# Sample tokens of a hybrid decoder layer: convolution states moved as whole rows, memory attention with four heads in 32-column strips

## The chip, the cores and the metric

The kernel runs on one core of one Trainium2 chip. The metric is the device time of one execution in microseconds (us). The engines are named as in the profile: PE (TensorE matmul), PEld (TensorE weight load), DVE (VectorE), ACT (ScalarE), POOL (GpSimd, which also issues the gathers of expert rows) and SP (SyncE, which issues all other DMAs, one after another in the order of its program). L12 is line 12 of the kernel before, unless a line of the changed kernel is named.

## The reference

One decoder layer with shared weights for 1024 prompt tokens and 8 sample tokens. The change concerns the sample tokens alone:

```python
def _causal_dwconv(u, buf, w, b):
    full = jnp.concatenate([buf.astype(u.dtype), u], axis=1)
    out = lax.conv_general_dilated(full, w[:, None, :], (1,), 'VALID', ..., feature_group_count=u.shape[-1])
    return out + b, full[:, full.shape[1] - (w.shape[0] - 1):]
...
xbc_c, new_ssd_buf = _causal_dwconv(xbc, ssd_buf, ssd_conv_w, ssd_conv_b)        # 3 old rows, 3072 channels
cv, new_conf_buf = _causal_dwconv(glu, conf_buf, conf_conv_w, conf_conv_b)       # 30 old rows, 1024 channels
sc = jnp.einsum('blhd,bmhd->bhlm', qh, mem_k) * (MEM_HEADDIM ** -0.5)            # 4 heads of 256, 256 memory tokens
pr = jax.nn.softmax(sc, axis=-1)
o = jnp.einsum('bhlm,bmhd->blhd', pr, mem_v)
```

For each sample token both convolutions read a state of old rows and give back the state shifted by one row with the new row at its end. In the memory attention each of the 8 samples has keys and values of its own (4 heads, 256 tokens, 256 features: 1 MB of keys and 1 MB of values per sample).

## The kernel before, in words

The prompt runs in four groups of 128, 128, 384 and 384 tokens (called G0 to G3 here). `main(G)` works on feature-major blocks of 128 features: each product loads a 512 KB block of weights into the pool `wr` (four buffers, `load_raw`, L167) and multiplies it. In G2 and G3 the block is first split on chip into two float32r parts by ACT (`wh`, L175) and DVE (`wl`, L177), so that its buffer is free again after the split; the products with `wso`, `wmo` and `wco` use it raw on PE (L197).

Between the products the program emits, at a fixed pace, rows of the expert layer of earlier groups: POOL gathers a 512 KB set of expert vectors into `uv` (L404), DVE multiplies them (L413, L423). The order of every engine's queue is fixed when the program is built; nothing is reordered at run time.

The sample tokens ride with G1 in the input projection (their columns land in `proj_s`). The rest of their first half, `samples()`, is a generator. Its first step runs behind G1, one step more after each input product of G2, and what is left over is emitted by `drain()` in the first half of G3 (L565). A scheduler then moves what it can forward: the first convolution's steps stand in the queues of G1's memory attention.

- First convolution (L880 to L896): three pieces of 8 channel blocks. Each loads the old rows into `win[..., 0:3]`, POOL writes the new row into `win[..., 3]`, DVE does four taps, and SP stores `win[..., 1:4]`. In `win` a row of a channel and a sample has four floats, in memory three, so that each load and store moves runs of 12 bytes: 128 x 64 of them, 96 KB.
- Second convolution (L943 to L955): eight blocks with 31 taps; `wn` holds 31 floats where memory holds 30, so that runs are 120 bytes, 128 x 8 per transfer.
- Memory attention (`sample_attention`, L970): for each head and sample a 256 KB load into the pool `sb` (four buffers), then two products of an 8-column block with 256 columns (`zq` holds a sample's query in one column and zeros in the others, so that the samples' products add up in one PSUM tile of 8 partitions). Heads go in pairs: scores of 16 loads, softmax over 8 partitions, then the values likewise.

On the chip the first convolution runs from about 691 us, the second from 1578 us, the keys from 1669 us. The values' products, and all but three of their loads, stand in G3 at 2320 to 2356 us.

Of the kernel before, what the change touches and what calls it, by code (L numbers as in the profile page):

```python
# [18 lines left out]
P = 128  # L19
D = 1024  # L20
# [47 lines left out]
def hybrid_layer(ctx: ExitStack, tc, I, O):  # L68
# [145 lines left out]
    def tick(n=1, work=bg):  # L214
        """Emits the next n steps of the work that fills the gaps."""
# [19 lines left out]
    def behind():  # L235
        """The vector engine's instruction LAG before the last that is not one of the experts' rows."""
# [7 lines left out]
    def spread():  # L244
        """Emits the experts' next rows that are due, behind the vector engine's work up to here."""
# [50 lines left out]
    def layer_norm_f(xs, nt):  # L296
        """Centres and scales feature-major blocks in place."""
# [22 lines left out]
    def route(pn, ntb, heads, sv, si, idx, gate, ij=None):  # L320
        """sv, si: for each half [pn, ntb, heads, 16], the best keys; idx, gate [pn, ntb, heads*16]."""
# [21 lines left out]
        # gates  # L343
# [9 lines left out]
        # ranks in both halves from the position: a < 4: a*16 + b; a >= 4: 64 + (a-4)*4 + b  # L353
# [33 lines left out]
    def layer_norm2(r, pn, junk, rows=None):  # L387
        """Token-major [pn, D] in place: the last normalisation."""
# [18 lines left out]
    def peer_experts(pn, ns, x1, idx, gate, acc):  # L407
        """acc [pn, D] = sum over the ns slots of gate * gelu(x1 . u) * v."""
# [33 lines left out]
    def front(g):  # L442
        """Loads a group's tokens, splits them, and works out the step sizes of its state space."""
# [6 lines left out]
        G.nx = nx = nt + NS if g == RIDE else nt    # the sample tokens ride with an early group  # L450
        G.no = nt + NS if G.last else nt            # and, from their mixers on, with the last
# [35 lines left out]
    def out_product(G, src, xs, f, name, add=False):  # L487
        """An output block; the sample columns go to S[name]."""
# [11 lines left out]
    def pack(G, srcs, scale=None, s=None):  # L500
        """The operands of an output product, in the last group with the sample columns s behind them."""
# [12 lines left out]
    def main(G):  # L514
# [24 lines left out]
        # -- state space branch, the convolution branch's blocks between its products  # L539
        ms, squares = None, []  # L540

        def sums(n):
            """The sums over the squares of the first n quarters."""
# [49 lines left out]
        # -- attention to the memory  # L593
# [50 lines left out]
        # -- the convolution branch's rest  # L644
# [8 lines left out]
        # -- output projection and residual  # L653
# [12 lines left out]
    def norm1(G):  # L666
        """The first normalisation."""
# [6 lines left out]
    def keep_tokens(G):  # L674
        """Token-major copies for the experts."""
# [9 lines left out]
    def routing(G):  # L685
        """The tokens' experts and gates, in steps."""
# [37 lines left out]
    def softplus_dt(ps, pn, nt):  # L724
        """dt = softplus(ps + bias), da = -exp(a_log) * dt; [pn, nt, 32]."""
# [10 lines left out]
        dve.scalar_tensor_tensor(w, u, -1.0, e, op0=OP.add, op1=OP.subtract)   # (u-1) - e  # L736
# [119 lines left out]
    def sample_mixers():  # L856
        # step sizes
# [21 lines left out]
        # convolution of x, B, C  # L879
# [3 lines left out]
        for j0 in (0, 8, 16):  # L883
            js = slice(j0, j0 + 8)
            win = sb()[:, :256].rearrange("p (j b t) -> p j b t", j=8, b=8)
            sp.dma_start(win[:, :, :, 0:3], I["sconv"][:, js])
            pool.tensor_copy(win[:, :, :, 3], proj_s[:, 16 + j0:24 + j0])
            for i in range(4):
                w = cw[:, js, i].unsqueeze(2).to_broadcast([P, 8, 8])
                if i == 0:  # L890
                    dve.tensor_tensor(xc[:, js], win[:, :, :, 0], w, op=OP.mult)
                else:
                    dve.tensor_tensor(tmp[:, js], win[:, :, :, i], w, op=OP.mult)
                    dve.tensor_tensor(xc[:, js], xc[:, js], tmp[:, js], op=OP.add)
            sp.dma_start(O["sconv"][:, js], win[:, :, :, 1:4])
            yield  # L896
# [4 lines left out]
        # state update  # L901
# [40 lines left out]
        # convolution branch  # L942
# [3 lines left out]
        cv = proj_s[:, 40:48]  # L946
        for j in range(8):
            wn = sb()[:, :8 * TAPS].rearrange("p (b t) -> p b t", b=8)
            sp.dma_start(wn[:, :, 0:30], I["fconv"][:, j])
            dve.tensor_tensor(wn[:, :, 30], proj_s[:, 40 + j], sg[:, j], op=OP.mult)  # L950
            sp.dma_start(O["fconv"][:, j], wn[:, :, 1:31])
            pr = sb()[:, :8 * TAPS].rearrange("p (b t) -> p b t", b=8)
            dve.tensor_tensor(pr, wn, cw_[:, j].unsqueeze(1).to_broadcast([P, 8, TAPS]), op=OP.mult)
            dve.tensor_reduce(cv[:, j], pr, axis=AX.X, op=OP.add)
            yield  # L955
        dve.tensor_tensor(cv, cv, cc[:, C_FB:C_FB + 8].unsqueeze(2).to_broadcast([P, 8, 8]), op=OP.add)
# [9 lines left out]
    def diagonal(z, first, n):  # L966
        """The diagonals of n of the [8, 8] squares of z."""
        return z[:, first * 64:(first + n) * 64].rearrange("p (f k) -> p f k", k=64)[:, :, 0:64:9]

    def sample_attention():  # L970
        qs = proj_s[:, 56:64]
        act.activation(qs, qs, AF.Copy, scale=1.0 / 16)
        # each sample's query stands alone in its column, so that the samples' products add up
# [3 lines left out]
        zp = None  # L977
        for h0 in (0, 2):
            psc = psm()[:8].rearrange("p (h m) -> p h m", h=2)
            for h in range(2):  # L980
                for b in range(8):
                    k = sb().rearrange("p (a b) -> p a b", a=2)
                    sp.dma_start(k, I["ck"][b, h0 + h])
                    for i in range(2):
                        o = (2 * (h0 + h) + i) * 64 + b * 8
                        pe.matmul(psc[:, h], zq[:, o:o + 8], k[:, i], start=(b + i == 0), stop=(b + i == 8))
                    yield
            stt = sm([8, 3, 2], "s_stt")
            dve.tensor_reduce(stt[:, 0], psc, axis=AX.X, op=OP.max)
            dve.tensor_scalar(stt[:, 1], stt[:, 0], -1.0, None, op0=OP.mult)  # L990
            pr = sb()[:8].rearrange("p (h m) -> p h m", h=2)
            for h in range(2):
                act.activation(pr[:, h], psc[:, h], AF.Exp, bias=stt[:, 1, h:h + 1], accum_out=stt[:, 2, h:h + 1])
            dve.reciprocal(stt[:, 2], stt[:, 2])
            for h in range(2):
                act.activation(pr[:, h], pr[:, h], AF.Copy, scale=stt[:, 2, h:h + 1])
            pt = psm()
            for h in range(2):
                for mb in range(2):
                    o = (2 * h + mb) * 8  # L1000
                    pe.transpose(pt[:, o:o + 8], pr[:, h, mb * P:(mb + 1) * P], ident[:8, :8])
            if zp is None:
                zp = sm([P, 512], "s_zp")
                pool.memset(zp, 0.0)
            act.activation(diagonal(zp, 2 * h0, 4), pt[:, 0:32].rearrange("p (f b) -> p f b", f=4), AF.Copy)
            yield
        os_ = proj_s[:, 56:64]
        for h0 in (0, 2):
            po = psm()[:8].rearrange("p (h d) -> p h d", h=2)
            for h in range(2):  # L1010
                for b in range(8):
                    v = sb().rearrange("p (a b) -> p a b", a=2)
                    sp.dma_start(v, I["cv"][b, h0 + h])
                    for mb in range(2):
                        o = (2 * (h0 + h) + mb) * 64 + b * 8
                        pe.matmul(po[:, h], zp[:, o:o + 8], v[:, mb], start=(b + mb == 0), stop=(b + mb == 8))
                    yield
            o8 = sb()[:8]
            act.activation(o8, po.rearrange("p h d -> p (h d)"), AF.Copy)
            pt = psm()  # L1020
            for f in range(4):
                pe.transpose(pt[:, f * 8:(f + 1) * 8], o8[:, f * P:(f + 1) * P], ident[:8, :8])
# [348 lines left out]
```

## Time and profile before

| | us |
|---|---|
| median of 3 runs | 4752.73 |
| lowest, highest | 4751.45, 4761.79 |
| span of the profiled execution | 4755.2 |

The profiled execution has no run time beside its span; the span, first to last instruction, stands for it and lies 2.5 us over the median. Busy shares of that span: PE 85%, DVE 77%, ACT 38%, POOL 38%, the 16 DMA engines 80% (both queues of data together), at a mean granted TensorE clock of 0.908. No engine is full over the whole; which of them ends a wait changes from stage to stage, so the stages that the change touches have to be looked at one by one.

### The profile page before, as it was taken

Reading aid. Unit: us, or ns where it says so; the run is one execution under the profiler, and the core shown is the slowest. Engines: PE = TensorE matmul, PEld = TensorE weight load, DVE = VectorE, ACT = ScalarE, POOL = GpSimd, SP = SyncE. Lnnn points to the kernel's source line nnn. Section 1 sums busy time; section 2 is a strip of 40 time slices with the busy share of each in tenths; the row PEclk is TensorE's granted clock in tenths of the full one; section 3 lists DMA queues with packets and bytes.
Section 4 is the critical chain, followed back from the end, with each engine's and each line's share of the span. In section 5 each row is a group of like instructions: output and inputs, shape, how many; then the busy total and the mean of one; then the engine's idle time right before and its main releaser. Section 6 shows DMA issues by size and latency. Waiting matters only on the chain. (4 is left out here: it accounts for less than half of the span.)

```text
span 4755.2 us, 61836 instructions
## 1 busy us (share of the span) xinstructions
PE 4060.0 (85%) x20483; PEld 3296.9 (69%) x20483; DVE 3651.7 (77%) x7682; ACT 1809.1 (38%) x4128; POOL 1800.8 (38%) x1595
## 2 busy tenths in 40 slices
PE   9999961589878899899769898889887899789997
PEld 8999860578666776577448686545555688677886
DVE  1363561668898799789988899879886799788998
ACT  3434420136456332154225432221786333323334
POOL 0000030443533334554134644554111455555663
PEclk9999885889978999989888799889898999999999
DMA  6676689887847877987566876987567999999998
GB/s 200 211 237 223 204 275 52 306 306 258 289 158 233 260 272 268 359 280 251 180 230 209 322 250 221 339 298 266 189 216 268 323 389 389 255 349 366 371 383 300
DMA packets 500161, 1278.29 MB, mean 269 GB/s; under 512 B 111312, under 2 KB 182864, under 8 KB 497664
## 3 DMA queue, kind: packets, MB, share of 16 engines
q0 software_dynamic: 186880, 679.56, 40.7%
q1 hardware_dynamic: 312960, 594.77, 39.3%
q8 instruction: 162, 2.65, 0.2%
q14 instruction: 159, 1.30, 0.1%
HBM read 1220.22 MB, written 53.93 MB: 268 GB/s over the span
## 5 line engine op out<-in xcount | busy, mean ns | idle before, releaser
L404 POOL DMA_INDIRECT uv<-in_peer_u,idx x640 | 789.8, 1234 | 1198.4 <-DVE uv L413 804.5
L404 POOL DMA_INDIRECT uv<-in_peer_v,idx x640 | 841.7, 1315 | 899.6 <-DVE pacc L423 547.8
L413 DVE SCALAR_TENSOR_TENSOR uv<-uv,x 128x1024 f32<-128x1024 f32 (+1 forms) x656 | 789.5, 1218 | 198.9 <-DMA uv<-in_peer_u,idx 186.0
L423 DVE SCALAR_TENSOR_TENSOR pacc<-uv,av,pacc 128x1024 f32<-128x1024 f32 (+1 forms) x650 | 831.9, 1280 | 98.6 <-DMA uv<-in_peer_v,idx 87.4
L186 PE MATMUL mm<-xt,wh 128*128 128x384 f32 x2816 | 790.5, 361 | 22.5 <-ACT b L589 12.7
L197 PE MATMUL mm<-b,wr 128*128 128x128 f32 (+2 forms) x3072 | 746.6, 397 | 32.0 <-ACT b L648 9.9
L197 PEld LDWEIGHTS mm<-b,wr 128*128 128x128 f32 x3072 | 491.8, 200 | 239.5 <-issue 26.1
L175 ACT ACTIVATE wh<-wr 128x1024 fp32r<-128x1024 f32 x274 | 290.2, 1060 | 830.7 <-DMA wr<-in_win 250.1
L186 PEld LDWEIGHTS mm<-xt,wh 128*128 128x128 f32 x2816 | 538.8, 200 | 58.4 <-ACT b L589 17.6
L186 PE MATMUL mm<-xt,wl 128*128 128x384 f32 x1408 | 502.0, 357 | 36.0 <-DVE wl L177 35.9
L197 PE MATMUL mm<-xt,wr 128*128 128x128 f32 (+1 forms) x2816 | 371.7, 292 | 98.2 <-DMA wr<-in_win 91.3
L535 DVE SCALAR_TENSOR_TENSOR b<-raw,cc,b 128x128 f32<-128x128 f32 (+1 forms) x960 | 443.1, 478 | 11.7 <-ACT b L533 4.7
L197 PEld LDWEIGHTS mm<-xt,wr 128*128 128x128 f32 x2816 | 357.7, 204 | 107.7 <-issue 92.3
L177 DVE TENSOR_TENSOR wl<-wr,wh 128x1024 fp32r<-128x1024 f32 x274 | 333.3, 1217 | 32.7 <-ACT wh L175 32.2
L186 PEld LDWEIGHTS mm<-xt,wl 128*128 128x128 f32 x1408 | 280.7, 199 | 47.8 <-DVE wl L177 42.0
L1223 PE MATMUL mm<-wh,b 128*128 128x512 f32 x768 | 246.0, 402 | 16.7 <-ACT b L150 16.4
L150 ACT ACTIVATE b<-acc 128x384 fp32r<-128x384 f32 x128 | 66.7, 525 | 372.7 <-PE st L1223 224.5
L186 PE MATMUL sp<-b,wh 128*128 128x384 f32 x784 | 206.2, 345 | 0.5 <-ACT b L682 0.5
L186 PE MATMUL tp<-b,wh 128*128 128x384 f32 x784 | 202.6, 340 | 0.0
L1162 PEld LDWEIGHTS mm<-e,e 128*128 128x128 f32 x768 | 119.9, 208 | 95.1 <-ACT e L1161 83.8
L1223 PE MATMUL ss<-wh,b 128*128 128x512 f32 x512 | 182.9, 398 | 0.0
L197 PE MATMUL mm<-acc,wr 128*128 128x128 f32 (+3 forms) x640 | 153.0, 402 | 27.0 <-DVE acc L591 12.7
(386 smaller groups left out, 6880.1 us busy)
## 6 DMA issues: line engine op xcount, KB each, us to landing
wr<-in_win SPq DMA_DIRECT2D x352, 512.0 KB, 4.6
wr<-in_peer_ut SPq DMA_DIRECT2D x128, 512.0 KB, 7.1
e<-in_peer_v SPq DMA_DIRECT2D x256, 256.0 KB, 7.2
wr<-in_wso SPq DMA_DIRECT2D x64, 512.0 KB, 4.8
wr<-in_wq SPq DMA_DIRECT2D x64, 512.0 KB, 5.5
gd<-xt SPq DMA_DIRECT2D x16, 1536.0 KB, 5.1
xt<-gd SPq DMA_DIRECT2D x16, 1536.0 KB, 18.9
wr<-in_wmo SPq DMA_DIRECT2D x32, 512.0 KB, 5.2
```

Source lines behind the costliest of these rows:

```text
L150: act.activation(hi, src, AF.Copy)
L175: act.activation(wh, wr, AF.Copy)
L177: dve.tensor_tensor(wl, wr, f32(wh), op=OP.subtract)
L186: pe.matmul(ps, a[:, k], b[k0 + k], start=(i == 0), stop=(i == n - 1))
L197: pe.matmul(ps, w[:, k], xs[k], start=(k == 0), stop=(k == 7))
L404: pool.indirect_dma_start(out=dst, out_offset=None, in_=table, in_offset=bass.IndirectOffsetOnAxis(ap=idx_col, axis=0))
L413: dve.scalar_tensor_tensor(u, u, 1.0, x1, op0=OP.mult, op1=OP.mult, accum_out=av[:, s:s + 1])
L423: dve.scalar_tensor_tensor(acc, v, av[:, s:s + 1], acc, op0=OP.mult, op1=OP.add)
L535: dve.scalar_tensor_tensor(cv, raw[:, i:i + nt], col(C_FW, j * TAPS + i), cv, op0=OP.mult, op1=OP.add)
L1162: pe.matmul(pg[:, u * P:(u + 1) * P], oj[:, u], oi[:, u], start=True, stop=True)
L1223: pe.matmul(outs[2 * tbk + dh], a[:, ts], v[:, dh * 512:dh * 512 + 512], start=(c == 0 and i == 0), stop=(c == P - 1 and i == 2))
```

## The change

Three parts, all on the sample tokens:

- First convolution: a piece loads its old rows into a tile `old` of the layout of memory (768 bytes in a row of a partition, one run). POOL copies taps 1 and 2 into a tile `new` of the same layout and the new row behind them, and `new` is stored whole. The fourth tap multiplies the new row in place.
- Second convolution: likewise with 960 bytes per partition; the gate product of all eight blocks is one instruction ahead of the loop, and the 31st tap two instructions behind it.
- Memory attention: a step takes one sample with all four heads. Two loads of 512 KB (two heads each) go into the pool `wr`, the four buffers of the weights. Head h's product goes to PSUM partitions 32h to 32h+7, so that one PSUM tile holds all four heads; softmax and transposes run once, over 128 partitions. Keys and values need 17 steps of the generator where they needed 68, so that nothing of them is left for G3.

```diff
         for j0 in (0, 8, 16):
             js = slice(j0, j0 + 8)
-            win = sb()[:, :256].rearrange("p (j b t) -> p j b t", j=8, b=8)
-            sp.dma_start(win[:, :, :, 0:3], I["sconv"][:, js])
-            pool.tensor_copy(win[:, :, :, 3], proj_s[:, 16 + j0:24 + j0])
-            for i in range(4):
+            old, new = (sb()[:, :192].rearrange("p (j b t) -> p j b t", j=8, b=8) for _ in range(2))
+            sp.dma_start(old, I["sconv"][:, js])
+            pool.tensor_copy(new[:, :, :, 0:2], old[:, :, :, 1:3])
+            pool.tensor_copy(new[:, :, :, 2], xc[:, js])
+            sp.dma_start(O["sconv"][:, js], new)
+            dve.tensor_tensor(xc[:, js], xc[:, js], cw[:, js, 3].unsqueeze(2).to_broadcast([P, 8, 8]), op=OP.mult)
+            for i in range(3):
                 w = cw[:, js, i].unsqueeze(2).to_broadcast([P, 8, 8])
...
-            sp.dma_start(O["sconv"][:, js], win[:, :, :, 1:4])
...
+        glu, cv = proj_s[:, 40:48], sg
+        dve.tensor_tensor(glu, glu, sg, op=OP.mult)
         for j in range(8):
-            wn = sb()[:, :8 * TAPS].rearrange("p (b t) -> p b t", b=8)
-            sp.dma_start(wn[:, :, 0:30], I["fconv"][:, j])
-            dve.tensor_tensor(wn[:, :, 30], proj_s[:, 40 + j], sg[:, j], op=OP.mult)
-            sp.dma_start(O["fconv"][:, j], wn[:, :, 1:31])
-            pr = sb()[:, :8 * TAPS].rearrange("p (b t) -> p b t", b=8)
-            dve.tensor_tensor(pr, wn, cw_[:, j].unsqueeze(1).to_broadcast([P, 8, TAPS]), op=OP.mult)
+            old, new, pr = (sb()[:, :240].rearrange("p (b t) -> p b t", b=8) for _ in range(3))
+            sp.dma_start(old, I["fconv"][:, j])
+            pool.tensor_copy(new[:, :, 0:29], old[:, :, 1:30])
+            pool.tensor_copy(new[:, :, 29], glu[:, j])
+            sp.dma_start(O["fconv"][:, j], new)
+            dve.tensor_tensor(pr, old, cw_[:, j, 0:30].unsqueeze(1).to_broadcast([P, 8, 30]), op=OP.mult)
             dve.tensor_reduce(cv[:, j], pr, axis=AX.X, op=OP.add)
             yield
+        dve.tensor_tensor(glu, glu, cw_[:, :, 30].unsqueeze(2).to_broadcast([P, 8, 8]), op=OP.mult)
+        dve.tensor_tensor(cv, cv, glu, op=OP.add)
...
+        def heads(ps, z, src, b):
+            ts = []
+            for h0 in (0, 2):
+                t = wp.tile([P, 2, 2, 256], F32, name="wr", bufs=WRB)
+                sp.dma_start(t, src[b, h0:h0 + 2].rearrange("h p i m -> p h i m"))
+                ts.append(t)
+            for i in range(2):
+                for h in range(4):
+                    o = (2 * h + i) * 64 + b * 8
+                    pe.matmul(ps[32 * h:32 * h + 8], z[:, o:o + 8], ts[h // 2][:, h % 2, i],
+                              start=(b + i == 0), stop=(b + i == 8))
+
+        psc = psm()[:, :256]
+        dve.memset(psc, 0.0)
+        for b in range(8):
+            heads(psc, zq, I["ck"], b)
+            yield
...
+        po = psm()[:, :256]
+        dve.memset(po, 0.0)
+        for b in range(8):
+            heads(po, zp, I["cv"], b)
+            yield
```

How the queues move. SP's queue at the first convolution, before (names are destination tile, then source; x2 is two in a row):

```order
L169 DMA wr<-in_win 128x1024 x3
L886 DMA sb<-in_sconv 128x64x3
L895 DMA out_sconv<-sb 128x64x3
L169 DMA wr<-in_win 128x1024
L886 DMA sb<-in_sconv 128x64x3 x2
L169 DMA wr<-in_win 128x1024
L895 DMA out_sconv<-sb 128x64x3 x2
```

and of the change:

```order
L169 DMA wr<-in_win 128x1024 x3
L886 DMA sb<-in_sconv 128x192
L889 DMA out_sconv<-sb 128x192
L169 DMA wr<-in_win 128x1024
L886 DMA sb<-in_sconv 128x192
L169 DMA wr<-in_win 128x1024
L886 DMA sb<-in_sconv 128x192
L889 DMA out_sconv<-sb 128x192 x2
```

The six transfers keep their places among the weight loads; their shape goes from 128 x 64 runs of 3 to 128 rows of 192, and the third load goes behind one more weight load.

SP's queue in G2's memory attention and merge, before:

```order
L169 DMA wr<-in_wmo 128x1024
L983 DMA sb<-in_ck 128x512
L169 DMA wr<-in_win 128x1024 x3
L169 DMA wr<-in_wmo 128x1024
L169 DMA wr<-in_win 128x1024
L983 DMA sb<-in_ck 128x512 x2
L169 DMA wr<-in_wmo 128x1024
```

and of the change:

```order
L169 DMA wr<-in_win 128x1024 x2
L985 DMA wr<-in_cv 128x2x512 x2
L169 DMA wr<-in_win 128x1024
L985 DMA wr<-in_cv 128x2x512 x2
L169 DMA wr<-in_wmo 128x1024
L169 DMA wr<-in_win 128x1024
```

Where one load of 256 KB into `sb` stood beside a product's weights, two of 512 KB into `wr` stand now; all keys and values are loaded within 16 such steps of G2.

PE's queue in the first half of G3, ahead of the first products with `wso`, before (L1016 is the values' product, L547 sums squares):

```order
L840 MATMUL tp<-ident,e_17938 128x128 x4
L547 MATMUL st<-b,ones 128x384 x3
L1001 MATMUL sp<-ident,sb 128x8 x4
L1016 MATMUL sp<-sb,s_zp 8x256 x32
L1022 MATMUL sp<-ident,sb 128x8 x4
L1016 MATMUL sp<-sb,s_zp 8x256 x32
L1022 MATMUL sp<-ident,sb 128x8 x4
L547 MATMUL st<-b,ones 128x384 x2
L197 MATMUL mm<-b,wr 128x392 x8
```

and of the change:

```order
L186 MATMUL mm<-xt,wl 128x384
L840 MATMUL tp<-ident,e_18041 128x128 x4
L547 MATMUL st<-b,ones 128x384 x5
L197 MATMUL mm<-b,wr 128x392 x8
L547 MATMUL st<-b,ones 128x384 x2
```

The 64 products of the values, in two blocks of 32, are gone from there.

## Rows read from the trace of the kernel before

**Rows 1.** Page: span, and GB/s in 40 slices of 118.9 us.

```profile
span 4755.2 us, 61836 instructions
GB/s 200 211 237 223 204 275 52 306 306 258 289 158 233 260 272 268 359 280 251 180 230 209 322 250 221 339 298 266 189 216 268 323 389 389 255 349 366 371 383 300
```

**Rows 2.** Stretches: start:end, length, busy us (instructions) per engine, clock, DMA share, GB/s.

```profile
core 0: us, PE busy (x) PEld busy (x) DVE busy (x) ACT busy (x) POOL busy (x), PEclk, DMA share, GB/s
650.00:675.00 25.00, 20.64 (x151) 19.42 (x152) 19.63 (x56) 3.00 (x15) 11.70 (x13) 0.93 1.03 409
711.00:750.00 39.00, 0.00 (x0) 0.00 (x0) 0.77 (x4) 0.00 (x0) 0.00 (x0) 0.52 1.29 32
764.00:842.00 78.00, 0.00 (x0) 0.00 (x0) 9.87 (x24) 0.89 (x3) 8.26 (x7) 0.52 1.39 63
700.00:925.00 225.00, 70.61 (x499) 65.92 (x498) 93.91 (x281) 26.79 (x81) 52.15 (x46) 0.67 1.18 147
```

**Rows 3.** Waits from 700 to 860 us: total us, times, longest.

```profile
PE mm L197 <- DMA wr<-in_win: 79.4, 2, 78.8
...
DVE proj_s L891 <- DMA sb<-in_sconv: 43.2, 2, 41.9
...
PE ss L613 <- ACT b L601: 40.3, 1, 40.3
```

**Rows 4.** SP's queue from 700 us: start, us to issue, what.

```profile
703.49 23.25 SPq L169 DMA_DIRECT2D wr<-in_win  x1
...
752.18 25.40 SPq L895 DMA_DIRECT2D out_sconv<-sb  x2
777.63 53.96 SPq L169 DMA_DIRECT2D wr<-in_win  x1
```

**Rows 5.** DMA of the whole: packets; one issue line, us to landing.

```profile
DMA packets 500161, 1278.29 MB, mean 269 GB/s; under 512 B 111312, under 2 KB 182864, under 8 KB 497664
...
out_sconv<-sb SPq DMA_DIRECT2D x3, 96.0 KB, 85.2
```

**Rows 6.** DVE's waits from 1575 to 1660 us.

```profile
DVE sb L953 <- DMA sb<-in_fconv: 14.2, 4, 5.0
```

**Rows 7.** SP's queue's own waits from 1575 to 1660 us.

```profile
SPq L951 <- DMA sb<-in_fconv: 46.6, 8, 8.7
```

**Rows 8.** Stretches of G2 and G3, columns as in Rows 2.

```profile
1677.00:1810.00 133.00, 132.18 (x622) 99.21 (x622) 125.35 (x244) 49.66 (x102) 42.43 (x41) 1.00 0.72 248
1810.00:1886.00 76.00, 71.92 (x284) 45.66 (x285) 71.29 (x126) 21.98 (x33) 31.57 (x27) 0.98 0.84 290
2319.00:2392.00 73.00, 32.12 (x143) 10.89 (x141) 73.00 (x296) 4.09 (x8) 0.00 (x0) 0.77 0.35 105
```

**Rows 9.** Groups from 1677 to 1810 us: busy us, mean ns, idle before.

```profile
L177 DVE TENSOR_TENSOR wl<-wr,wh 128x1024 fp32r<-128x1024 f32 x17 | 20.7, 1216 | 1.6 <-ACT wh L175 1.5
L986 PE MATMUL sp<-sb 128*8 128x256 f32 x68 | 18.0, 380 | 0.7 <-DMA sb<-in_ck 0.7
L175 ACT ACTIVATE wh<-wr 128x1024 fp32r<-128x1024 f32 x17 | 17.9, 1056 | 47.3 <-PE mm L186 21.4 <-issue 18.8 <-DVE raw L528 6.1
...
L986 PEld LDWEIGHTS sp<-sb 128*8 128x8 f32 x68 | 4.5, 88 | 9.5 <-issue 6.0
```

**Rows 10.** DMA from 1677 to 1810 us, packets and one issue line.

```profile
DMA packets 10395, 32.95 MB, mean 248 GB/s; under 512 B 1138, under 2 KB 1394, under 8 KB 10387
...
wr<-in_win SPq DMA_DIRECT2D x14, 512.0 KB, 3.5
```

**Rows 11.** The same from 940 to 1000 us.

```profile
DMA packets 8201, 24.34 MB, mean 406 GB/s; under 512 B 915, under 2 KB 2668, under 8 KB 8197
...
wr<-in_win SPq DMA_DIRECT2D x7, 512.0 KB, 10.2
```

**Rows 12.** PE's longest wait from 2290 to 2420 us.

```profile
PE st L547 <- ACT b L559: 37.0, 1, 37.0
```

**Rows 13.** POOL's copies of L887: min/median/max ns, first and last start.

```profile
L887 POOL COPY sb<-proj_s x3: 292/298/774, 691.7 to 698.9; 128x64 f32<-128x64 f32 x3
```

More of the change, by code (lines that the diff above doesn't have):

```diff
@@ L884, in sample_mixers @@
             js = slice(j0, j0 + 8)
-            win = sb()[:, :256].rearrange("p (j b t) -> p j b t", j=8, b=8)
-            sp.dma_start(win[:, :, :, 0:3], I["sconv"][:, js])
-            pool.tensor_copy(win[:, :, :, 3], proj_s[:, 16 + j0:24 + j0])
-            for i in range(4):
-                w = cw[:, js, i].unsqueeze(2).to_broadcast([P, 8, 8])
[L890 to L894, printed above, removed]
-            sp.dma_start(O["sconv"][:, js], win[:, :, :, 1:4])
+            old, new = (sb()[:, :192].rearrange("p (j b t) -> p j b t", j=8, b=8) for _ in range(2))
[5 more added lines that the diff above has]
+            for i in range(3):
+                w = cw[:, js, i].unsqueeze(2).to_broadcast([P, 8, 8])
+                dve.tensor_tensor(tmp[:, js], old[:, :, :, i], w, op=OP.mult)
+                dve.tensor_tensor(xc[:, js], xc[:, js], tmp[:, js], op=OP.add)
             yield
@@ L976, in sample_attention @@
         act.activation(diagonal(zq, 0, 8), qs, AF.Copy)
[L977 to L1005, printed above, removed]
-            yield
@@ L1007, in sample_attention @@
-        os_ = proj_s[:, 56:64]
[L1008 to L1022, printed above, removed]
-            act.activation(os_[:, 2 * h0:2 * h0 + 4], pt[:, 0:32].rearrange("p (f b) -> p f b", f=4), AF.Copy)
-            yield
+        def heads(ps, z, src, b):
[9 more added lines that the diff above has]
+                              start=(b + i == 0), stop=(b + i == 8))
@@ new lines, in sample_attention @@
+        psc = psm()[:, :256]
+        dve.memset(psc, 0.0)
+        for b in range(8):
+            heads(psc, zq, I["ck"], b)
+            yield
+        stt = sm([P, 3], "s_stt")
+        dve.tensor_reduce(stt[:, 0:1], psc, axis=AX.X, op=OP.max)
+        dve.tensor_scalar(stt[:, 1:2], stt[:, 0:1], -1.0, None, op0=OP.mult)
+        pr = sb()[:, :256]
+        act.activation(pr, psc, AF.Exp, bias=stt[:, 1:2], accum_out=stt[:, 2:3])
+        dve.reciprocal(stt[:, 2:3], stt[:, 2:3])
+        dve.tensor_scalar(pr, pr, stt[:, 2:3], None, op0=OP.mult)
@@ new lines, in sample_attention @@
+        pt = psm()
+        for mb in range(2):
+            pe.transpose(pt[:, mb * P:(mb + 1) * P], pr[:, mb * P:(mb + 1) * P], ident)
+        zp = sm([P, 512], "s_zp")
+        pool.memset(zp, 0.0)
+        for mb in range(2):
+            act.activation(zp.rearrange("p (h m k) -> p h m k", h=4, m=2)[:, :, mb, 0:64:9],
+                           pt[:, mb * P:(mb + 1) * P].rearrange("p (h b) -> p h b", h=4)[:, :, 0:8], AF.Copy)
+        yield
+        po = psm()[:, :256]
+        dve.memset(po, 0.0)
@@ new lines, in sample_attention @@
+        for b in range(8):
+            heads(po, zp, I["cv"], b)
+            yield
+        o8 = sb()[:, :256]
+        act.activation(o8, po, AF.Copy)
+        pt = psm()
+        os_ = proj_s[:, 56:64]
+        for db in range(2):
+            pe.transpose(pt[:, db * P:(db + 1) * P], o8[:, db * P:(db + 1) * P], ident)
+        for db in range(2):
+            act.activation(os_[:, db:8:2], pt[:, db * P:(db + 1) * P].rearrange("p (h b) -> p h b", h=4)[:, :, 0:8],
+                           AF.Copy)
```

1 line of the change is left out of this document (removed).

## The prediction

> **What bounds the kernel now.** I read first the page's row of GB/s over the span [rows 1]: one slice of 40 moves 52 GB/s where its neighbours move 275 and 306. It lies at 713 to 832 us, where the first convolution of the sample tokens loads and stores its state. Then the table of stretches [rows 2]: PE does nothing from 711 to 750 us and nothing from 764 to 842 us, and DVE, ACT and POOL nearly nothing (DVE 0.8 and 9.9 us), while the DMA engines are taken all the time (share 1.29 and 1.39) for 32 and 63 GB/s. Just before, they moved 409 GB/s. So the DMA engines are busy with pieces too small to carry anything, and every engine waits for them. The list of waits [rows 3] gives the size: PE waits 40.3 us for a copy by ACT, while DVE waits 41.9 us in one piece for the old rows, and 78.8 us for a block of weights. SP's queue [rows 4] shows why the weights are late: two weight loads take 23.25 and 53.96 us to be issued, and the last two stores 25.40, since the queue ahead is full. A store of 96 KB takes 85.2 us to land [rows 5].
>
> Second, G2's memory attention and merge (1677 to 1810 us): PE is busy 132.2 of 133 us, DVE 125.4, DMA moves 248 GB/s [rows 8]. Whatever is put on PE there costs its length. Third, the values in G3 (2319 to 2392 us): PE is busy only 32.1 of 73 us, DVE all 73.0 [rows 8], and PE then waits 37.0 us for ACT's squares of what DVE finishes last [rows 12].
>
> **The change part by part.**
>
> First convolution, removed: the two stops of PE, 40.3 + 78.8 = 119.1 us [rows 3]. They come back whole only if nothing else fills the stretch. Over 700 to 925 us, 225 us, DVE has 93.9 us of work, PE 70.6, and 33.1 MB moved (147 GB/s x 225), 81 us at 409 GB/s [rows 2]. Without the stops 106 us are left, 12 more than DVE needs, so that they can go. But in the stops 39 x 32 + 78 x 63 = 6.2 MB came in ahead, 15 us at 409 GB/s, which now have to run beside other work. Between 0 and 15 us are given back; I take 4, since 106 us have room for them. What replaces the six transfers is 128 runs of 768 bytes each, and DVE's first tap still waits for a landing: a transfer lands in 3.5 us with DMA lightly used [rows 10] and in 10.2 with it full [rows 11]. One is exposed at least in part, three at most, so 0 to 31 us; I take 5, for one. POOL's copies cost some 0.3 us each, the duration of a copy of 64 elements [rows 13], and POOL is idle three quarters of that stretch [rows 2]; without that cover six copies would be 2 us. Behind a store that waits for POOL, SP holds a weight load; that is part of the 31 us.
>
> Second convolution: DVE waits 14.2 us in all for the loads of 120-byte runs [rows 6], and SP stands 46.6 us behind them before it can store [rows 7]. With runs of 960 bytes I take 5 us off. The bounds are 14 us off and 14 us more: `old`, `new` and `pr` take three of the four `sb` buffers per block, where two stood before, and the store now waits for POOL, whose copies stand behind gathers; two copies more per block, which POOL's idle time hides.
>
> Keys and values on PE: before, 68 instructions of 256 columns take 18.0 us in the window [rows 9], 0.265 us each; two instructions are one product. Now all 128 products (256 instructions) run there. One after another they take 67.8 us, four strips at once 17. No row shows strips at other partitions, so these are the bounds. What goes: the 18.0 us there, and after it the other 60 instructions of the keys (128 less 68), 15.9 us, at a place where PE is busy 71.9 of 76 us [rows 8]. Net: +34 us one after another, -17 us at four at once. I take the middle, 2 at a time: 33.9 - 33.9 = 0, because two instructions of a product stay in one strip and only those of neighbours can run side by side.
>
> The Trainium skill, TensorE: Matmul & The Clock Gate (What overlaps and what doesn't), says that a weight load runs beside products in flight only where their row groups differ, which speaks against strips, as all four use the same rows. The row of weight loads (88 ns each [rows 9]) is for one strip and does not decide it. By that rule 256 x 0.088 = 22.5 us would be added (an estimate), and the forecast below would be 4671; the 2.38 times that the same page gives for three column strips (Measured speedup vs the span model) would make the 67.8 us 28, and the forecast 4643.
>
> Keys and values in the weights' buffers: a step takes two of the four `wr` buffers. A weight block has to land, be copied by ACT (1.06 us) and split by DVE (1.22 us) [rows 9]: 5.8 us at a landing of 3.5, 12.5 us at 10.2. The steps come every 133/17 = 7.8 us, 17 being the visits that 68 instructions make at four each. The window's 32.95 MB grow by 16 x 1.05 MB less the 17 x 0.26 MB that were there, to 45.3 MB or 341 GB/s, between 248 and 406 GB/s [rows 10, 11]; in proportion a landing is then 7.4 us and the chain 9.7, 1.9 us over a step. With one block loaded ahead nothing shows; with none, 1.9 us at each of 16 steps, 30 us; with DMA full, 4.7 us or 75. I take a third of 30, 10 us, since two buffers are left for the weights.
>
> Values in G3: 64 products go from PE, 36 us from 2320 to 2356. They lie under DVE's 73.0 us of routing, which ends last there, and the order keeps that routing ahead of the rows PE waits for. I take 0; all 36 would be the bound if DVE's rows were not what is waited for. What is late next is the same wait for ACT, longer by what PE no longer does.
>
> Sum: -119 + 4 + 5 - 5 + 0 + 10 + 0 = -105 us. From the profiled execution's 4755.2 that is 4650; the median of the runs is 2.5 us below that span, so I forecast 4648.
>
> **The rivals.**
>
> Strips one after another: K/V cost +34 instead of 0, 4682. For it: no row shows two products at once. Against: they write different partitions and don't wait for each other.
>
> Slower: the weights of G2 are loaded with nothing ahead. Then a step needs the full landing, ACT and DVE (12.5 us) and, before its buffers are free, the K/V products of the step before (67.8/16 = 4.2 us), 16.7 us instead of 7.8: 16 x 8.9 = 142 us, less the 10 already in the sum, 4780. It decides from 105/16 = 6.6 us per step beyond what the sum has. For it: SP issues in order, and K/V loads that wait for PE stand ahead of weights. Against: in this window ACT's copies wait mostly for PE, not for loads [rows 9], so there is slack ahead.
>
> The values' burst counts: 36 us more, 4612. For it: PE runs nothing else at 2320 to 2356. Against: DVE's 73.0 of 73 [rows 8].
>
> The change does not do what it says: the runs stay short, and the stops stay, 4753. Against: the new queue shows transfers of 128 rows of 192.
>
> **How the numbers follow.** Chances: forecast (gain 75 to 135 us) 0.74, strips one after another 0.14, burst 0.07, slower 0.03, short runs stay 0.02. About 0.2% (9.5 us) is what a measurement can tell from none. So faster 0.95, same 0.02, slower 0.03. The range: with the uncertain terms at their good ends (5 less for the loads, 9 for the second convolution, 17 for strips, 10 for the buffers) it is 4607; at the bad end strips one after another with half of the upper bound for the buffers (34, and 38 instead of 10) give 4710. I take 4610 to 4705.
>
> **What would show it.** Right: no stretch without PE near 711 to 842 us, the 40-slice row without its 52, and packets under 512 bytes down by 6 x 8192 + 16 x 1024 = 65,536 to about 45,800 [rows 5]. K/V products: 256 instructions between about 1550 and 1710 us of the new trace, whose starts lie 0.12 us apart if two run at once, 0.2 or more if none do. PE's wait at the squares of G3 grows from 37 to about 73 us. Wrong: ACT's or PE's waits for weights of more than 30 us in G2, or SP's stores waiting for POOL by more than 10 us a piece, or a new idle stretch of DVE near 700 us.

## The result and the profile after

The changed kernel takes 4653.0 us (median of four runs, 4643.5 to 4662.6), the kernel before on the same chip 4757.3: 0.9774 of the time, 95% interval 0.9754 to 0.9795, 104 us less. The profiled execution of the changed kernel spans 4660.8 us, 94.4 less than that of before.

The page of the changed kernel: the 40-slice row of GB/s, and the packets. The seventh slice, 52 GB/s before [rows 1], stands at 315, and 66,048 packets under 512 bytes are gone (65,536 were forecast).

```profile
span 4660.8 us, 61736 instructions
...
GB/s 198 208 238 232 202 296 315 339 247 275 207 184 275 278 286 317 317 227 244 106 236 225 325 249 231 371 279 265 182 218 290 341 387 368 250 356 354 364 386 304
DMA packets 436928, 1278.27 MB, mean 274 GB/s; under 512 B 45264, under 2 KB 119632, under 8 KB 434432
```

The stretches around the first convolution, columns as in [rows 2], and PE's longest wait from 680 to 830 us. Between 711 and 750 us PE was busy 0 us and is now busy 32.9, and DVE 35.9 of 39. What is late next is DVE: PE waits 22.1 us, 20.3 of them in one piece, for rows of the prompt's own convolution (L535).

```profile
711.00:750.00 39.00, 32.87 (x239) 30.77 (x239) 35.87 (x113) 12.30 (x36) 19.23 (x17) 0.91 0.93 340
764.00:842.00 78.00, 42.91 (x308) 40.02 (x306) 56.17 (x127) 14.56 (x43) 43.27 (x38) 0.80 0.94 353
700.00:925.00 225.00, 163.65 (x1110) 154.37 (x1108) 170.86 (x420) 62.63 (x150) 106.43 (x102) 0.86 0.90 331
```

```profile
PE st L300 <- DVE b L535: 22.1, 2, 20.3
```

Where the time went is read from how far an instruction that no edit touches stands ahead in the other trace. This table is worked out from the start times of one such line, ACT's copies in L525, k-th against k-th; the heads are times of before, the last two rows are runs told below.

```
start before, us     708   859  1288  1650  1709  1752  1778  1810  2424  2863
changed kernel        -3  -121  -123  -132  -125  -113  -101   -95   -95   -92
e1_conv               -7  -125  -137  -143  -143  -141  -141  -141  -134  -133
e2_att                -5    -6    -8    -7    +1   +12   +20   +26   +20   +19
```

A single entry is good to some 10 us: from 859 to 1288 us, where no edit sets the changed kernel and e1_conv apart, they gain 2 and 12. The first convolution gives 118 us, the second some 9, no more than that uncertainty, and between 1650 and 1810 us of before, where the keys and values are loaded and multiplied, 37 of them are lost again (32 to 42 in each run below that loads them in such steps). Nothing moves in G3. The same program stretch (from the copy of L533 at 1661 us of before to 1810) takes 149 us before and 187 after; columns as in [rows 2].

```profile
1661.00:1810.00 149.00, 145.34 (x703) 111.27 (x703) 140.06 (x273) 58.57 (x117) 48.73 (x48) 1.00 0.74 257
```

```profile
1528.00:1715.00 187.00, 166.90 (x917) 123.49 (x916) 150.63 (x292) 55.23 (x115) 65.16 (x59) 0.95 0.84 295
```

PE's idle time grows from 3.7 to 20.1 us. Of it 11.1 us are waits for weights (5.7 for ACT's copies, 3.4 for DVE's splits, 2.0 for blocks that PE takes raw) and 4.3 for keys and values to land. ACT's and SP's waits in this stretch say why (total, times, longest). Before, ACT's copies waited there mostly for PE [rows 9]. Now ACT waits 79.8 us for weights to land, and SP stands 68.0 us before loads of keys and values (51.5 before the change), and 20.1 before loads of weights (none before), until PE has multiplied an earlier sample.

```profile
PE mm L186 <- ACT wh L175: 5.7, 3, 2.9
PE sp L990 <- DMA wr<-in_ck: 3.4, 1, 3.4
PE mm L186 <- DVE wl L177: 3.4, 4, 1.5
...
ACT wh L175 <- DMA wr<-in_win: 79.8, 15, 13.7
...
SPq L985 <- PE sp L990: 68.0, 12, 11.1
SPq L985 <- DVE wl L177: 29.6, 9, 12.7
SPq L169 <- DVE wl L177: 24.9, 8, 8.3
SPq L169 <- PE sp L990: 20.1, 3, 12.2
```

The other 21.6 us are in PE's busy time (145.3 to 166.9). The keys' and values' instructions take 24.3 us (12.8 and 11.5) where 68 took 18.0 [rows 9]. Ten instructions of L300, 4 us, and 16 more of L186 (447 where there were 431), some 5 us, now lie inside the stretch. And what is left of L186 and L197 takes some 8 us longer, at a mean granted clock of 0.95 instead of 1.00 (the upper of its two levels, 2.4 GHz). Before and after:

```profile
L186 PE MATMUL mm<-xt,wh 128*128 128x384 f32 x287 | 78.8, 351 | 0.0
L186 PE MATMUL mm<-xt,wl 128*128 128x384 f32 x144 | 49.4, 343 | 1.8 <-DVE wl L177 1.8
```

```profile
L186 PE MATMUL mm<-xt,wh 128*128 128x384 f32 x298 | 84.9, 365 | 5.9 <-ACT wh L175 5.7
L186 PE MATMUL mm<-xt,wl 128*128 128x384 f32 x149 | 54.0, 363 | 3.5 <-DVE wl L177 3.4
...
L990 PE MATMUL sp<-wr,sb 128*8 128x256 f32 x128 | 12.8, 402 | 3.5 <-DMA wr<-in_ck 3.4
...
L990 PE MATMUL sp<-wr,s_zp 128*8 128x256 f32 x128 | 11.5, 380 | 0.9 <-DMA wr<-in_cv 0.9
```

The clock is lower where PE has stood still: in PE's timeline two instructions of L186 take 0.51 us before a wait of 2.93 us, and 0.84 after it.

```profile
1600.76 0.51 PE L186 MATMUL mm<-xt,wh 128*128 128x384 f32 x2
1601.11 0.34 PE L186 MATMUL mm<-xt,wl 128*128 128x384 f32 x1
1601.54 1.04 PE L990 MATMUL sp<-wr,sb 128*8 128x256 f32 x12
1605.51 0.45 PE L186 MATMUL mm<-xt,wh 128*128 128x384 f32 x1 [2.93 <-ACT wh L175]
...
1608.35 0.84 PE L186 MATMUL mm<-xt,wh 128*128 128x384 f32 x2
```

The strips themselves do all that was hoped where a sample's 16 instructions stand together. PE's timeline before: four instructions in one strip, 1.03 us.

```profile
1750.32 1.03 PE L986 MATMUL sp<-sb 128*8 128x256 f32 x4
```

After: sixteen in four strips, 1.05 us. In the trace they start in fours, 0.007 us apart, and the next four 0.215 us later.

```profile
1641.38 0.34 PE L186 MATMUL mm<-xt,wl 128*128 128x384 f32 x1
1641.65 1.05 PE L990 MATMUL sp<-wr,s_zp 128*8 128x256 f32 x16
```

In G3 PE's wait for the squares is 73.6 us where it was 37.0 [rows 12]:

```profile
PE st L547 <- ACT b L559: 73.6, 1, 73.6
```

### The profile page after: what moved, and what is told of

It reads as the page before. It is cut to its first block, busy times and chain, and to the rows that moved or that the text cites. A ratio compares the mean times of both kernels' runs of the same rounds, so it can differ in the third digit from the quotient of the medians.

```text
span 4660.8 us, 61736 instructions
## 1 busy us (share of the span) xinstructions
PE 4028.7 (86%) x20471; PEld 3289.6 (71%) x20471; DVE 3651.9 (78%) x7677; ACT 1798.8 (39%) x4112; POOL 1822.1 (39%) x1614
## 4 chain that ended last, share of the span: by engine, by line
issue 18%; DMA 15%; DVE 12%; PE 11%; POOL 8%; ACT 5%; POOLq 0%; SPq 0%; DVEq 0%; ACTq 0%
POOL uv L404 8%; DMA uv<-in_peer_v,idx 8%; DMA uv<-in_peer_u,idx 3%; PE mm L186 3%; DVE uv L413 2%; DVE pacc L423 2%; PE mm L197 2%; ACT xt L1169 2%; DVE b L535 2%; ACT e L1164 2%; DVE wl L177 1%; PE sp L186 1%; PE mm L1226 1%; DMA e<-in_peer_v 1%; DMA wr<-in_win 1%
## 5 line engine op out<-in xcount | busy, mean ns | idle before, releaser
L404 POOL DMA_INDIRECT uv<-in_peer_u,idx x640 | 800.9, 1251 | 1151.4 <-DVE uv L413 825.9
L404 POOL DMA_INDIRECT uv<-in_peer_v,idx x640 | 832.2, 1300 | 916.5 <-DVE pacc L423 571.9
L186 PE MATMUL mm<-xt,wh 128*128 128x384 f32 x2816 | 793.2, 362 | 30.1 <-ACT wh L175 15.1
L197 PE MATMUL mm<-b,wr 128*128 128x128 f32 (+2 forms) x3072 | 747.8, 398 | 38.1 <-ACT b L648 14.4
L197 PEld LDWEIGHTS mm<-b,wr 128*128 128x128 f32 x3072 | 492.5, 201 | 241.0 <-issue 22.7
L186 PEld LDWEIGHTS mm<-xt,wh 128*128 128x128 f32 x2816 | 541.0, 200 | 67.7 <-ACT wh L175 19.6
L186 PE MATMUL mm<-xt,wl 128*128 128x384 f32 x1408 | 505.3, 360 | 44.5 <-DVE wl L177 44.3
L535 DVE SCALAR_TENSOR_TENSOR b<-raw,cc,b 128x128 f32<-128x128 f32 (+1 forms) x960 | 444.6, 479 | 11.7 <-ACT b L533 4.7
L197 PE MATMUL mm<-xt,wr 128*128 128x128 f32 (+1 forms) x2816 | 368.5, 290 | 18.8 <-DMA wr<-in_win 8.9
L197 PEld LDWEIGHTS mm<-xt,wr 128*128 128x128 f32 x2816 | 354.3, 202 | 28.3 <-issue 11.9
L186 PEld LDWEIGHTS mm<-xt,wl 128*128 128x128 f32 x1408 | 281.6, 200 | 61.1 <-DVE wl L177 53.5
L186 PE MATMUL tp<-b,wh 128*128 128x384 f32 x784 | 206.9, 346 | 0.0
L186 PE MATMUL sp<-b,wh 128*128 128x384 f32 x784 | 203.5, 341 | 0.5 <-ACT b L682 0.5
L753 POOL COPY halo<-raw 128x3 f32<-128x3 f32 x96 | 51.0, 532 | 323.8 <-ACT raw L751 323.1
```

What stands on the lines that cost most here:

```text
L186: pe.matmul(ps, a[:, k], b[k0 + k], start=(i == 0), stop=(i == n - 1))
L404: pool.indirect_dma_start(out=dst, out_offset=None, in_=table, in_offset=bass.IndirectOffsetOnAxis(ap=idx_col, axis=0))
L535: dve.scalar_tensor_tensor(cv, raw[:, i:i + nt], col(C_FW, j * TAPS + i), cv, op0=OP.mult, op1=OP.add)
```

## The experiments

### The parts alone

e1_conv has both convolutions of the change and the attention of before, e8_first the first convolution alone, e2_att the attention alone:

```diff
 # e1_conv, against the changed kernel
-        def heads(ps, z, src, b):
...
+        for h0 in (0, 2):
+            psc = psm()[:8].rearrange("p (h m) -> p h m", h=2)
...
 # e8_first: the same, and also
-            old, new, pr = (sb()[:, :240].rearrange("p (b t) -> p b t", b=8) for _ in range(3))
...
+            wn = sb()[:, :8 * TAPS].rearrange("p (b t) -> p b t", b=8)
...
 # e2_att: before, with sample_attention() of the changed kernel
```

> Both convolutions changed, the attention as before. Theory A (the convolutions gave all of the gain and more, and the new attention gives some 35 us of it back in G2, because weights come late behind the keys' and values' loads): the trace of the changed kernel is 117 to 121 us ahead after the first convolution and 130 to 133 after the second, so 4757 - 130 = 4627 us, 4618 to 4636. Theory B (the sum on record was right term by term: convolutions -115, keys and values +10): 4642 us. Theory C (the attention brings a gain of its own): 4660 or more.

> The attention alone changed, the convolutions as before. Theory A: slower than before by 25 to 45 us, 4782 to 4802, and ACT waits some 80 us for weights between the second convolution and the end of the values, where it waited for PE before. Theory B: +10, 4767 us. Theory C: faster than before, 4740 or less.

> The first convolution alone changed, the second and the attention as before. If the first gives 117 to 121 us and the second some 9 (its share in the trace of the changed kernel): 4636 us, 4630 to 4642. If the second gives nothing of its own: 4620 to 4627, as e1_conv.

> e1_conv again, in more rounds, as the version that beats both: 4615 to 4630 us, at least 20 us below the changed kernel's 4653.

Measured, each against the kernel before on the same chip: e1_conv 4621.5 us, 0.9724 (0.9697 to 0.9751), and again as e11_conv5 in five rounds 4624.3 us, 0.9730 (0.9711 to 0.9749), an interval that lies below the changed kernel's. e8_first 4633.9 us, 0.9753 (0.9717 to 0.9789), in its first range. e2_att 4787.2 us, 1.008 (1.005 to 1.011). So the first convolution is worth 117 to 120 us (by the ratio, by the medians), the second some 10 to 14 more (their intervals overlap, so that this is not clear of noise), and the attention costs 21 to 32 with the convolutions changed and 32 to 38 without. Theory A holds, theories B and C fall. In e2_att the loss lies in the same place (the table above), and ACT waits for weights there too, 73.8 us:

```profile
ACT wh L175 <- DMA wr<-in_win: 73.8, 14, 10.7
```

### What costs in the attention

e3_noload keeps every product and leaves out the loads, so that the sample tokens' attention is computed from a constant table:

```diff
-            ts = []
-            for h0 in (0, 2):
-                t = wp.tile([P, 2, 2, 256], F32, name="wr", bufs=WRB)
-                sp.dma_start(t, src[b, h0:h0 + 2].rearrange("h p i m -> p h i m"))
-                ts.append(t)
...
-                    pe.matmul(ps[32 * h:32 * h + 8], z[:, o:o + 8], ts[h // 2][:, h % 2, i],
+                    pe.matmul(ps[32 * h:32 * h + 8], z[:, o:o + 8], cc[:, 0:256],
```

> The changed kernel without the loads of keys and values: the 256 instructions of its strips read a constant table instead, so that the sample tokens' attention is not the reference's. PE's work stays the same. Theory A: what is given back in G2 comes with the loads (their two of four weight buffers, SP's wait for PE, the DMA traffic) and not from the products, which take 0.066 us each in a full row of 16: 4653 - 37 = 4616 us, 4605 to 4625, and ACT's wait for weights in the stretch falls from 80 us to under 20. Rival (the strips' instructions and their changes of place between the groups' products cost PE the time): 4645 to 4655 us.

Measured 4627.9 us, 0.9742 (0.9716 to 0.9768), 3 us above theory A's range. The program stretch takes 152 us instead of 187, with 256 instructions of keys and values in it where before had 68, and they need 19.0 us; ACT waits for PE again:

```profile
1527.00:1679.00 152.00, 146.87 (x887) 113.12 (x886) 138.10 (x271) 52.77 (x111) 50.30 (x47) 0.98 0.65 223
...
ACT wh L175 <- PE mm L186: 34.5, 8, 9.0
...
L985 PE MATMUL sp<-cc,sb 128*8 128x256 f32 x128 | 9.8, 410 | 0.9 <-ACT sb L979 0.9
L985 PE MATMUL sp<-cc,s_zp 128*8 128x256 f32 x128 | 9.2, 380 | 0.0
```

So the loads cost 35 of the 38 us (187 less 152), not the strips. But the whole program is no faster than e1_conv, which multiplies one head after another: with free loads the strips bring nothing that can be told from noise. Theory A had left out why. Of the keys' 60 instructions that followed the window before, 20 stood ahead of 1857 us, 32 in the gap of the layer norm (1857 to 1886 us), where DVE is busy 25.4 of 29 us, and the last 8 at 2112 us. Without the 32 the gap is as long. The same stretch before and after:

```profile
1857.00:1886.00 29.00, 24.92 (x82) 11.56 (x81) 25.39 (x48) 14.85 (x24) 15.17 (x11) 0.94 0.85 297
```

```profile
1756.00:1785.00 29.00, 17.25 (x36) 8.87 (x35) 27.06 (x51) 15.58 (x24) 13.74 (x11) 0.71 0.67 216
```

PE's own products at the end of the gap became slower, too: with PE idle for 12 of its 29 us the granted clock is 0.71 where it was 0.94, and 16 instructions of L197 take 8.32 us instead of 5.43, behind a wait for ACT:

```profile
1881.05 5.43 PE L197 MATMUL mm<-b,wr 128*128 128x384 f32 x16
```

```profile
1778.59 8.32 PE L197 MATMUL mm<-b,wr 128*128 128x384 f32 x16 [4.53 <-ACT b L648]
```

Three ways to load otherwise follow. e4_sb loads each head into a small buffer as before the change; e7_poolqueue does that from POOL's queue; e10_wrpool keeps the weights' buffers and only issues from POOL.

```diff
 # e4_sb
-                t = wp.tile([P, 2, 2, 256], F32, name="wr", bufs=WRB)
-                sp.dma_start(t, src[b, h0:h0 + 2].rearrange("h p i m -> p h i m"))
+                t = sb().rearrange("p (i m) -> p i m", i=2)
+                sp.dma_start(t, src[b, h])
...
-        zq = sb()
+        zq = sm([P, 512], "s_zp")
 # e7_poolqueue, against e4_sb
-                sp.dma_start(t, src[b, h])
+                pool.dma_start(t, src[b, h])
 # e10_wrpool, against the changed kernel
-                sp.dma_start(t, src[b, h0:h0 + 2].rearrange("h p i m -> p h i m"))
+                pool.dma_start(t, src[b, h0:h0 + 2].rearrange("h p i m -> p h i m"))
```

> The changed kernel with each head's keys and values in the four small buffers (sb, as before the change), and the weights alone in theirs; the same 16 instructions per sample in four strips. If the lack of weight buffers is what costs (two of four held): most of 37 us comes back, 4620 to 4630 us. If it is the order in SP's queue (a sample's loads wait for PE's products of the sample before, and the next weights stand behind them): little comes back, 4640 to 4660 us, and ACT still waits 50 us or more for weights in the stretch.

> As e4_sb, but the keys' and values' loads are issued by POOL, so that no weight load stands behind them in SP's queue. Theory (SP's order makes weights and next loads late): most of what e4_sb lost comes back, 4605 to 4628 us, and PE waits under 5 us for keys and values. Rival (POOL now waits for PE with the experts' gathers behind it, and DVE for them): 4640 us or more, with DVE's wait for rows of the experts grown by 15 us or more in the stretch.

> The changed kernel with one edit: POOL issues the keys' and values' loads, still into two of the four weight buffers. If SP's order (weights behind loads that wait for PE) was what cost: 4620 to 4635 us. If the buffers were (two of four held until PE has multiplied): 4645 to 4660 us, and ACT still waits 50 us or more for weights between the second convolution and the end of the values.

Measured: e4_sb 4652.4 us, 0.979 (0.9743 to 0.9837); e7_poolqueue 4652.1 us, 0.9788 (0.9757 to 0.9818); e10_wrpool 4643.6 us, 0.9772 (0.9751 to 0.9793). None differs from the changed kernel by more than the intervals, and the stretch takes 183, 183 and 181 us. They lose it in two ways. In e10_wrpool ACT still waits 62.4 us for weights, and SP 77.7 us for PE to free a weight buffer, although no load of keys stands in its queue:

```profile
ACT wh L175 <- DMA wr<-in_win: 62.4, 12, 12.8
...
SPq L169 <- PE sp L990: 77.7, 10, 13.7
```

So it is the buffers that cost there, and the order in SP's queue is not needed for it: its first expectation falls, and its second holds in ACT's wait, with the time 1.4 us below its range. In e7_poolqueue the weights have their four buffers and a queue of their own, and ACT no longer waits for them, though nearly as many bytes move (283 GB/s in the stretch, 295 in the changed kernel's): the traffic alone does not make weights late.

```profile
ACT wh L175 <- issue: 56.1, 7, 13.0
ACT wh L175 <- PE mm L186: 31.8, 9, 9.0
```

But four small buffers hold one sample, PE comes to it while heads are still landing, and the strips do not fill (in the trace's second step the four heads start at 0, 1.1, 2.7 and 4.3 us, where they start together once all have landed):

```profile
L990 PE MATMUL sp<-sb,s_zp 128*8 128x256 f32 x256 | 36.2, 391 | 14.0 <-DMA sb<-in_ck 9.6 <-DMA sb<-in_cv 4.1
```

36.2 us instead of 19.0 is what strips cost that are half filled, and 14.0 us of waits come on top: 31 us, as much as the stretch is longer than e3_noload's (183 less 152). Its first expectation falls (PE waits 14 us, not under 5), and its rival's reason too: DVE's waits for the experts' rows are 14.2 us, where the changed kernel has 9.7. e4_sb has the same 36.2 us, with waits of 11.6; its time is that of its second expectation, but not with ACT waiting for weights. What the three have in common is that a megabyte per sample has no second place to land in, beside the weights, while PE works on the first. That more buffers would bring the time back is argued from these waits and not shown: no run has more.

### The order of the products

```diff
-            for i in range(2):
-                for h in range(4):
+            for h in range(4):
+                for i in range(2):
```

> The changed kernel with the two loops of the products exchanged: both products of a head stand one behind the other, so that neighbours lie in one strip, where four neighbours lay in four strips. Theory (strips overlap because neighbours in PE's order go to different strips; a product that meets its own strip at work stops those behind it): 16 instructions take 2.1 us instead of 1.05, PE loses 16 x 1.1 = 18 us in G2, 4660 to 4675 us. Rival (each strip has a queue of its own, the order does not matter): 1.05 us for 16, 4648 to 4658 us.

Sixteen instructions take 1.07 us in this order too, still in fours, 0.013 us apart:

```profile
1643.36 1.07 PE L990 MATMUL sp<-wr,s_zp 128*8 128x256 f32 x16
```

The spacing, which was 0.007 us, says that the exchange reached the chip. So the theory falls: neighbours need not lie in different strips. Were products started strictly in the order of the program, the strips would wait for each other (2.1 us by the expectation); PE went on with other strips instead. The sentence ahead of the prediction that nothing is reordered at run time does not hold for them. The rival's 1.05 us holds, its time does not: 4669.8 us, 0.9827 (0.979 to 0.9865), is in the theory's range, but not by its mechanism. By the starts of L528 at 1661 and 1815 us of before the stretch loses 42 us, where the changed kernel loses 39. The profiled spans differ by 8 us, in no single place, and the interval meets the changed kernel's. Whether this kernel is slower, and by what, is left open.

### Loads and stores of the first convolution

e5_loads changes the three loads of before, e9_stores the three stores:

```diff
 # e5_loads
-            sp.dma_start(win[:, :, :, 0:3], I["sconv"][:, js])
+            old = sb()[:, :192].rearrange("p (j b t) -> p j b t", j=8, b=8)
+            sp.dma_start(old, I["sconv"][:, js])
+            pool.tensor_copy(win[:, :, :, 0:3], old)
 # e9_stores
-            sp.dma_start(O["sconv"][:, js], win[:, :, :, 1:4])
+            new = sb()[:, :192].rearrange("p (j b t) -> p j b t", j=8, b=8)
+            pool.tensor_copy(new, win[:, :, :, 1:4])
+            sp.dma_start(O["sconv"][:, js], new)
```

> The kernel before with one edit in the first convolution: the three loads take whole rows and POOL copies them into the window; the three stores still go in runs of 12 bytes. Theory A (each of the six transfers of 8192 runs holds the DMA engines for its share of the 119 us, loads and stores alike): half of the gain, 4757 - 60 = 4697 us, 4685 to 4710; the first stop (40.3 us) goes, the second stays at 40 to 80. Rival 1 (the stores alone make weights late): 4715 or more. Rival 2 (the loads do, the stores run on beside the rest): 4640 or less.

> The mirror of e5_loads: the kernel before, with its three loads still in runs of 12 bytes, and the three stores in whole rows from a copy that POOL makes. In the trace of before, 49,583 runs took 98.6 per cent of 16 engines for 160 us, 51 ns of an engine a run, so that the 24,576 runs that are left would take 78 us of all 16. Theory A (the runs' number counts, and e5_loads lost more than its half because each load stood behind a store, one after the other): 40 to 70 us faster, 4685 to 4715 us. Rival 1 (the stores are the cause, the loads run on beside the rest): 4650 to 4665. Rival 2 (either kind is enough for the whole stop): 4725 or more.

Measured: e5_loads 4734.8 us, 0.9962 (0.9944 to 0.998), 20 us; e9_stores 4646.1 us, 0.9778 (0.9758 to 0.9797), 104 us. Both first theories fall, and rival 1 of both holds (e9_stores 4 us below its range): the stores are the stop, and the loads in runs of 12 bytes run on beside the rest. The two gains, 20 and 104 us, add up to 124, where e8_first has 117 to 120. From 711 to 750 us, where PE was busy 0 us [rows 2], it is busy 7.8 us in e5_loads and 25.2 in e9_stores:

```profile
711.00:750.00 39.00, 7.80 (x40) 7.24 (x40) 4.46 (x20) 3.35 (x10) 2.03 (x5) 0.59 1.31 36
```

```profile
711.00:750.00 39.00, 25.16 (x168) 23.31 (x167) 30.99 (x95) 11.65 (x34) 21.13 (x20) 0.82 0.93 278
```

In e5_loads, from 690 to 800 us, the packets of SP's queue (nearly all runs of the stores) take 113.1% of 16 engines, 1990 us in sum for 24,657, or 81 ns each:

```profile
q1 hardware_dynamic: 24657, 2.07, 113.1%
```

In e9_stores, from 690 to 735 us, as many runs of the loads, with more weights among them, take 436 us in sum for 26,064 packets, 17 ns each:

```profile
q1 hardware_dynamic: 26064, 4.26, 60.5%
```

A share over 100% says that packets overlap: it is the time that packets take, not work of the engines alone. The trace's records of single packets, picked by their 12 bytes, leave the weights out. The 24,576 stored runs of e5_loads take 71 ns in the mean but 9 in the median: a tenth of them holds 81% of the time, and the longest takes 3.9 us. The 24,576 loaded runs of e9_stores take 9.5 ns in the mean and 9 in the median. In sum that is 109 us of all 16 engines for the stores and 15 for the loads. So most stored runs are as quick as loaded ones, and a few stand long; what these wait for, no run shows.

In e5_loads the whole-row loads stand behind the stores, and POOL waits for them:

```profile
POOL sb L888 <- DMA sb<-in_sconv: 78.4, 2, 41.2
...
PE mm L197 <- DMA wr<-in_wmo: 33.9, 1, 33.9
PE tp L623 <- DVE b L620: 33.7, 1, 33.7
```

The Trainium skill, DMA: Bandwidth & Descriptors (Specifications), says that a transfer below 512 bytes makes the DMA engine read, modify and write. It gives no direction; here the price is on the runs written to DRAM, in the mean seven times that of the runs read from it (71 and 9.5 ns), and no run shows the reading and modifying itself.

## Why the prediction was right

The time forecast, 4648, is 5 us from the measured 4653, and that it is so near is luck: the two convolutions brought 126 to 133 us where the sum has 115, and the attention cost 21 to 32 where it has 10. These terms were mis-sized in opposite directions, and a third hid that one of its parts could not be had.

**First convolution, -119 + 4 + 5.** Right in place and in size, -120 by e8_first, and in part in mechanism. Nothing of the 4 us for work that came in ahead is seen, nor of the 5 for exposed loads: POOL waits for a landing once, and DVE has other work. The argument put the stops down to pieces too small; that they were those of the stores was not in it, and its first stop was read as a wait for the loads [rows 3], which it was, but behind stores. The DMA shares of 1.29 and 1.39 [rows 2], read as engines taken all the time, count packets that overlap and in part stand.

**Second convolution, -5.** 6 to 9 us in traces, 10 to 14 between e8_first and e1_conv, neither clear of noise; the mechanism is the one named: DVE's wait for the loads is 5.7 us, where it was 14.2 [rows 6].

```profile
DVE sb L953 <- DMA sb<-in_fconv: 5.7, 5, 2.4
```

**Keys and values on PE, 0.** This step failed twice over, and its 0 is right by luck: e3_noload, which has the strips with nothing to load, lies 4 to 6 us above e1_conv's two sets of runs, within their intervals. "2 at a time" is four at once, 17 us for 256 instructions if nothing breaks them up, which was the good bound; its reason, that only neighbours in different strips run side by side, falls with e6_order. And the 15.9 us that should go after the window went only in part: 32 of those 60 instructions lay in a gap that DVE sets, and 8 at 2112 us, outside the 76. The step took PE's 71.9 of 76 us as one place; split at 1857 us it is a stretch that PE bounds and one that it does not. The Trainium skill, TensorE: Matmul & The Clock Gate (What overlaps and what doesn't), lets a weight load run beside products only where the row groups differ. Here 16 weight loads of 88 ns on the same rows begin within 0.46 us, where 1.4 would be needed one after another, so the trace does not agree. The factor of 2.38 for three strips (Measured speedup vs the span model) is 3.9 here for four, 4.12 us (four times 1.03) against 1.05.

**Weight buffers, +10.** The step that was most wrong. "Two buffers are left for the weights" was taken as a third of 30 us; it cost 37 in the stretch, some 2.3 us at each of 16 steps. The sign that the prediction gave for being wrong, ACT waiting more than 30 us for weights in G2, did show, with 79.8. What the estimate left out is that two buffers per sample stay taken until PE has multiplied, so that a weight load waits for PE's place in the program and not only for a landing, and that the products behind PE's pauses ran at the lower clock.

**Values in G3, 0.** As forecast: 73.6 us of wait for 73, and -95 us before and after the burst's place in the table.

Of the rivals, strips one after another and the burst that counts did not occur. The slower one, weights with nothing loaded ahead, is the mechanism that did, at 2.3 us a step instead of 8.9: below the 6.6 us from which it would have decided. The order in SP's queue, which spoke for it, is not what it needs (e10_wrpool).

e1_conv, the convolutions without the attention, beats both kernels: 4621 and 4624 us in its two sets of runs, 126 to 133 less than before and some 21 to 32 less than the changed kernel.

## What to carry to other kernels

A store in runs of a few bytes holds up every transfer behind it; shift on the chip and store whole rows, and where only one direction can be mended, the stores. Column strips multiply the products' pace by the number of strips only if all of a step's operands are there at once, so count the buffers that hold them, and what those buffers did before, ahead of PE's time. And before PE's saved time is booked, split the stretch at each place where PE waits for another engine: what ran in such a gap was free.

## What was not expected of the hardware

Four products in four 32-column strips of the array, on the same 128 rows, ran at 3.9 times the pace of one strip in float32, whichever way neighbours were ordered (1.05 and 1.07 us for 16). A run of 12 bytes took 71 ns in the mean when stored and 9.5 when loaded, with a median of 9 ns for both: a tenth of the stored runs held four fifths of their time.
